# An encoder layer on one core: the last two plain steps of a Strassen block taken together by output, a lag of four, the input loaded in smaller pieces

## Chip, core and metric

The kernel runs on one core of a Trainium2 chip. The metric is the device time of one launch in microseconds (us), the median of several runs. One core has TensorE (PE in the profile), VectorE (DVE), ScalarE (ACT), GpSimd (POOL) and SyncE (SP), which here issues the loads of weights and inputs. Each engine works through its own list of instructions; across engines, semaphores make one wait for the other.

## What is computed

One layer of an encoder on 256 tokens of 2048 features in float32: a gated feed-forward part, two attention mixers side by side with a gated merge, and a second feed-forward part, each with a norm ahead of it, a norm behind it, and a residual.

```python
def rmsnorm(x, g):
    xf = x.astype(jnp.float32)
    y = xf * lax.rsqrt(jnp.mean(xf * xf, axis=-1, keepdims=True) + EPS)
    return (y * g.astype(jnp.float32)).astype(x.dtype)

def swiglu(h, w_gate, w_up, w_down):
    return (jax.nn.silu(h @ w_gate) * (h @ w_up)) @ w_down
```

The hidden width of the feed-forward parts is 5632. The change touches how the products with `w_gate` and `w_up` are run, and the first product of each of the three parts.

## The kernel before

**Products.** Every float32 number is split in two parts of lower precision, a high part (ACT casts it, L178 for weights, L359 for activations) and a low part (DVE subtracts, L180 and L361). A product is then three matmuls: high by high, low by high, high by low (L201 to L203 in ordinary blocks, L259 to L261 in wide ones). One matmul takes 128 rows of K and gives 128 tokens by 512 columns. So every unit of weights that SP loads (1 MB of float32) goes through a cast on ACT and a split on DVE before PE can use it.

**Activations.** `pre(u, h)` of `make_xT` makes, for 256 features u and token half h, what the first block of a part needs: it applies the norm and residual of the part before (L424), transposes on PE (L352), casts on ACT (L359) and splits on DVE (L361). Each second u also gives a sum of squares (L371) for the norm, which is applied later by a factor.

**Ordinary blocks.** `run_block` gives 512 columns for both token halves. Step i multiplies u = i for half 0 and u = i - lag for half 1, so that half 1 runs `lag` steps behind. `lag` is LAG (3) where a part begins with activations that must first be made (the first mixer block, the first gate block of the second feed-forward part) and where the part before ends; it is 0 in the first gate block of all.

**Wide blocks.** `run_wide` gives 1024 columns at once: four outputs of 128 tokens by 512 columns, named P2, P3 (half 0), Q4 and X (half 1). In the gate and up blocks with odd number (1, 3, 5, 7, 9, in both feed-forward parts, 20 blocks) it mixes two kinds of steps, as `SKIND = "NSNSNSNN"` says: N is a plain step (24 matmuls for 256 features, six for each output), S is one step of Strassen's method, with seven products in place of eight on sums of activations (`forms`) and of weights (DVE L189 to L191). The products of all S steps gather in banks of PSUM; after the last S step, DVE combines them (L294 to L307): the product P1 is copied by ACT (a, L294), P2 gets a added (L295), and so on. Before the change two N steps follow the last S step, one after the other (block 1 of each part has its steps in another order, FIRST, and there only one N step follows). The first matmul of such a step adds to P2, and so has to wait until L295 is done. The output of a block leaves through `after` in the last step.

**What sets the order.** The code only names operations; a scheduler with priorities (`tc.high_priority`) and a queue of work put off (`later`, `pump`) sets the order on each engine when the kernel is built. Weights are asked for two units ahead (`LA`).

**Start.** At the top level, SP loads `x` in pieces of columns 0 to 256, 256 to 1024 and 1024 to 2048 for each half, and between them four quarters of the first unit of weights.

Of the kernel before, what the change touches and what calls it, by code (L numbers as in the profile page):

```python
# [29 lines left out]
NEG = -1e30  # L30
OFF_QA, OFF_KV, OFF_QB, OFF_KB, OFF_VB, OFF_GA, OFF_GB = 0, 1024, 1536, 2560, 3584, 4608, 6656
KU = D // (2 * P)
LAG = 3
LAG_END = 3
LA = 2
SKIND = "NSNSNSNN"
FIRST = (0, 2, 1, 4, 3, 6, 5, 7)
HP = 300
AHEAD = 2
PARTS = ((0, 3), (3, 7), (7, 11))  # L40
WARM = 7
# [3 lines left out]
def encoder_layer(  # L45
# [27 lines left out]
    def acc_tile():  # L73
        return accp.tile([P, NC], F32, tag="acc", name=nm("acc"))
# [121 lines left out]
    def weights(k):  # L196
        emit_upto(k + LA)
        return emitted[k]
# [28 lines left out]
    def run_block(start, nu, lhs, after, lag=0, pre=None, tail=None):  # L227

        acc = [acc_tile(), acc_tile()]
        for i in range(nu + lag):  # L230
            if pre is not None:
                if i == 0:
                    pre(0, 0)
                    if not lag:
                        pre(0, 1)
                if i + 1 < nu:
                    pre(i + 1, 0)
                k = i - lag if lag else i + 1
                if 0 <= k < nu:
                    pre(k, 1)  # L240
            if tail is not None and i == nu + lag - 1:
                tail(0, 0)
            for h, u in ((0, i), (1, i - lag)):
                if not 0 <= u < nu:
                    continue
                whi, wlo = weights(start + u // 2)
                t = lhs(u, h)
                for j in range(2):
                    q = 2 * (u % 2) + j
                    mm3(acc[h], t[:, 0, j, :], t[:, 1, j, :], whi[:, q, :], wlo[:, q, :],  # L250
                        u == 0 and j == 0, u == nu - 1 and j == 1)
                if u == nu - 1:
                    with tc.high_priority(HP):
                        after(h, 0, acc[h])
            if i % 2:
                pump()

    def mm3s(o, t, w, q, first, last, skip=False):
        nc.tensor.matmul(o, t[0], w[0][:, q, :], start=first, stop=False, skip_group_check=skip)  # L259
        nc.tensor.matmul(o, t[1], w[0][:, q, :], start=False, stop=False, skip_group_check=skip)  # L260
        nc.tensor.matmul(o, t[0], w[1][:, q, :], start=False, stop=last, skip_group_check=skip)  # L261

    def run_wide(block, lhs, forms, after):
# [3 lines left out]
        last_s = max([n for n, (_, k) in enumerate(steps) if k == "S"], default=-1)  # L267
        bank, opened = {}, set()
        end = len(steps) - 1

        def open_(o):
            if o not in bank:
                bank[o] = acc_tile()
            f = o not in opened
            opened.add(o)
            return f

        for n, (u, kind) in enumerate(steps):
            w = weights(start + n)
            if kind == "S":  # L280
# [10 lines left out]
                if n == last_s:  # L291
                    with tc.high_priority(HP):
                        a, u2, v = t2(), t2(), t2()
                        nc.scalar.copy(a, bank["P1"])  # L294
                        nc.vector.tensor_tensor(bank["P2"], bank["P2"], a, ALU.add)  # L295
                        nc.vector.tensor_tensor(u2, bank["P6"], a, ALU.add)
                        nc.vector.tensor_tensor(v, bank["Q5"], u2, ALU.subtract)
                        nc.vector.tensor_tensor(bank["P3"], bank["P3"], v, ALU.add)
                        nc.vector.tensor_tensor(u2, bank["P7"], u2, ALU.add)
                        if "X" in bank:  # L300
                            nc.vector.tensor_tensor(v, bank["Q5"], u2, ALU.subtract)
                            nc.vector.tensor_tensor(bank["X"], bank["X"], v, ALU.add)
                        else:
                            nc.vector.tensor_tensor(bank["P1"], bank["Q5"], u2, ALU.subtract)
                            bank["X"] = bank["P1"]
                            opened.add("X")
                        nc.vector.tensor_tensor(bank["Q4"], bank["Q4"], u2, ALU.add)  # L307
            else:
                order = (("P2", 0, 0), ("P3", 0, 1), ("X", 1, 1), ("Q4", 1, 0)) if last_s >= 0 else                     (("P2", 0, 0), ("P3", 0, 1), ("Q4", 1, 0), ("X", 1, 1))
                for o, h, c in order:  # L310
                    t = lhs(u, h)
                    for j in range(2):
                        f = open_(o)
                        closes = n == end or n == last_s - 1 and o == "X"
                        mm3s(bank[o], (t[:, 0, j, :], t[:, 1, j, :]), w, 2 * j + c, f, closes and j == 1, last_s >= 0)
                    if n == end:
                        with tc.high_priority(HP):
                            after(h, c, bank[o])
            pump()

    def half_of(t, u, h):
# [258 lines left out]
    for h in range(2):  # L580
        x_sb[h] = big([D], F32)
    load_x(0, 0, 256)
    load_unit(0, (0, 1))
    load_x(1, 0, 256)
    for h in range(2):
        load_x(h, 256, 1024)
    load_unit(0, (2, 3))
    for h in range(2):
        load_x(h, 1024, 2048)
    load_upto(2)  # L590
# [343 lines left out]
```

## Time and profile before

| | us |
|---|---|
| median of 3 runs | 2073.56 (2073.42 to 2074.51) |
| the profiled execution | 2074.24 |
| its span in the trace | 2072.5 |
| PE busy | 2036.4 (98%) |
| DVE busy | 1434.4 (69%) |
| ACT busy | 986.9 (48%) |

The profiled execution is 0.7 us above the median; 1.7 us of it lie outside the span. PE is the engine that hardly rests, so the time can be lowered only where PE rests, runs at a lower clock, or works without need. Its clock is 2.4 GHz where the granted clock is 1.00, and 1.2 GHz at 0.50.

### The profile page before, as it was taken

Reading aid. Unit: us, or ns where it says so; the run is one execution under the profiler, and the core shown is the slowest. Engines: PE = TensorE matmul, PEld = TensorE weight load, DVE = VectorE, ACT = ScalarE, POOL = GpSimd, SP = SyncE. Lnnn points to the kernel's source line nnn. Section 1 sums busy time; section 2 is a strip of 40 time slices with the busy share of each in tenths; the row PEclk is TensorE's granted clock in tenths of the full one; section 3 lists DMA queues with packets and bytes.
Section 4 is the critical chain, followed back from the end, with each engine's and each line's share of the span. In section 5 each row is a group of like instructions: output and inputs, shape, how many; then the busy total and the mean of one; then the engine's idle time right before and its main releaser. Section 6 shows DMA issues by size and latency. Waiting matters only on the chain. (4 is left out here: it accounts for less than half of the span.)

```text
span 2072.5 us, 22867 instructions
## 1 busy us (share of the span) xinstructions
PE 2036.4 (98%) x9193; PEld 1676.8 (81%) x9193; DVE 1434.4 (69%) x1413; ACT 986.9 (48%) x956; POOL 55.5 (3%) x91
## 2 busy tenths in 40 slices
PE   9999999999999999999999999999999999999997
PEld 6888887888878878888888888778888888888886
DVE  6984798647986675676665555659658885588854
ACT  7544555435554453455454344446345544455442
POOL 1000000000000010000000000000000000000000
PEclk9999999999999999999999999999999999999999
DMA  8556555666558546554545556546575655756672
GB/s 293 187 200 214 196 184 202 223 206 201 182 203 304 205 168 206 191 175 163 193 153 183 193 196 245 200 150 203 184 245 180 222 205 187 220 182 216 238 252 87
DMA packets 140570, 416.36 MB, mean 201 GB/s; under 512 B 8414, under 2 KB 9232, under 8 KB 139184
## 3 DMA queue, kind: packets, MB, share of 16 engines
q1 hardware_dynamic: 133872, 391.15, 54.7%
q0 software_dynamic: 6560, 23.75, 4.3%
q8 instruction: 72, 1.18, 0.2%
q14 instruction: 34, 0.28, 0.0%
q10 hardware_dynamic: 32, 0.01, 0.0%
HBM read 400.19 MB, written 14.68 MB: 200 GB/s over the span
## 5 line engine op out<-in xcount | busy, mean ns | idle before, releaser
L180 DVE TENSOR_TENSOR w<-raw,w 128x2048 fp32r<-128x2048 f32 (+3 forms) x376 | 797.1, 2125 | 482.3 <-ACT w L178 480.5
L178 ACT CAST w<-raw 128x2048 fp32r<-128x2048 f32 (+3 forms) x376 | 667.7, 1782 | 746.0 <-PE acc L260 580.3
L259 PE MATMUL acc<-w,xT 128*128 128x512 f32 x1368 | 537.0, 393 | 6.4 <-DVE acc L295 6.3
L260 PE MATMUL acc<-w,xT 128*128 128x512 f32 x1368 | 533.6, 390 | 0.0
L261 PE MATMUL acc<-w,xT 128*128 128x512 f32 x1368 | 515.5, 390 | 0.0
L260 PE MATMUL acc<-w,big 128*128 128x512 f32 x828 | 323.5, 391 | 0.0
L259 PE MATMUL acc<-w,big 128*128 128x512 f32 x828 | 322.7, 390 | 0.0
L261 PE MATMUL acc<-w,big 128*128 128x512 f32 x828 | 317.9, 390 | 0.2 <-DVE w L180 0.2
L259 PEld LDWEIGHTS acc<-w,xT 128*128 128x128 f32 x1368 | 256.8, 188 | 63.0 <-DVE acc L295 9.0
L261 PEld LDWEIGHTS acc<-w,xT 128*128 128x128 f32 x1368 | 256.9, 188 | 53.3
L260 PEld LDWEIGHTS acc<-w,xT 128*128 128x128 f32 x1368 | 256.9, 188 | 51.3
L261 PEld LDWEIGHTS acc<-w,big 128*128 128x128 f32 x828 | 155.4, 188 | 33.0 <-DVE w L180 1.3
L259 PEld LDWEIGHTS acc<-w,big 128*128 128x128 f32 x828 | 155.4, 188 | 32.5 <-ACT w L178 0.3
L260 PEld LDWEIGHTS acc<-w,big 128*128 128x128 f32 x828 | 155.5, 188 | 31.9
L178 ACT CAST big<-raw 128x2048 fp32r<-128x2048 f32 (+1 forms) x64 | 118.8, 1860 | 98.3 <-DVE raw L191 94.2
L180 DVE TENSOR_TENSOR big<-raw,big 128x2048 fp32r<-128x2048 f32 (+1 forms) x64 | 141.3, 2221 | 23.6 <-ACT big L178 18.0
L202 PE MATMUL acc<-w,xT 128*128 128x512 f32 x208 | 82.9, 402 | 4.2 <-DVE xT L361 4.0
L201 PE MATMUL acc<-w,xT 128*128 128x512 f32 x208 | 84.3, 408 | 1.6 <-ACT xT L359 1.6
L203 PE MATMUL acc<-w,xT 128*128 128x512 f32 x208 | 80.6, 398 | 0.1
L201 PE MATMUL acc<-w,big 128*128 128x512 f32 x192 | 74.4, 389 | 0.0
L202 PE MATMUL acc<-w,big 128*128 128x512 f32 x192 | 74.4, 389 | 0.0
L189 DVE TENSOR_TENSOR raw<-raw 128x1024 f32<-128x1024 f32 x60 | 73.4, 1223 | 1.1
(186 smaller groups left out, 1736.4 us busy)
## 6 DMA issues: line engine op xcount, KB each, us to landing
raw<-in_ffn_w_down SPq DMA_DIRECT2D x88, 1024.0 KB, 5.1
raw<-in_w_in SPq DMA_DIRECT2D x68, 1024.0 KB, 5.0
raw<-in_ffn_w_up SPq DMA_DIRECT2D x58, 1024.0 KB, 5.1
raw<-in_ffn_w_gate SPq DMA_DIRECT2D x57, 1024.0 KB, 5.6
raw<-in_ffn_w_gate SPq DMA_DIRECT2D x60, 512.0 KB, 4.7
raw<-in_ffn_w_up SPq DMA_DIRECT2D x60, 512.0 KB, 4.6
raw<-in_w_out SPq DMA_DIRECT2D x16, 1024.0 KB, 5.0
f_dram<-t POOLq DMA_DIRECT2D x32, 256.0 KB, 6.0
```

Of the source, the lines that this page charges most:

```text
L178: nc.scalar.copy(hi[:, sl], raw[:, sl])
L180: nc.vector.tensor_tensor(lo[:, sl], raw[:, sl], f32(hi[:, sl]), ALU.subtract)
L189: nc.vector.tensor_tensor(raw[:, 1::2], raw[:, 1:3], raw[:, 3:4].to_broadcast([P, 2, NC]), ALU.add)
L201: nc.tensor.matmul(o, lhi, rhi, start=first, stop=False)
L202: nc.tensor.matmul(o, llo, rhi, start=False, stop=False)
L203: nc.tensor.matmul(o, lhi, rlo, start=False, stop=last)
L259: nc.tensor.matmul(o, t[0], w[0][:, q, :], start=first, stop=False, skip_group_check=skip)
L260: nc.tensor.matmul(o, t[1], w[0][:, q, :], start=False, stop=False, skip_group_check=skip)
L261: nc.tensor.matmul(o, t[0], w[1][:, q, :], start=False, stop=last, skip_group_check=skip)
```

## The change

Three things are edited.

1. **`run_wide`.** The last two N steps (`joint`, wherever the last S step is third from the end: 18 of the 20 blocks) are run as one. The X part of the first of them comes first (6 matmuls), then P2, P3 and Q4, each with both steps (12 matmuls), then X of the second. The sum into X on DVE is put behind that first X part, and X now always has a bank of its own. Each output is handed to `after` when its own 12 matmuls are done.
2. **`run_block`.** LAG is 4. The calls of `pre` are made through `ahead`, one step earlier for half 1.
3. **The first loads.** x comes in columns 0 to 256, 256 to 512, 512 to 1024 and 1024 to 2048, and the quarters of the first weights are put between them otherwise.

```diff
--- before.py
+++ after.py
@@ -30,12 +30,13 @@
 NEG = -1e30
 OFF_QA, OFF_KV, OFF_QB, OFF_KB, OFF_VB, OFF_GA, OFF_GB = 0, 1024, 1536, 2560, 3584, 4608, 6656
 KU = D // (2 * P)
-LAG = 3
+LAG = 4
 LAG_END = 3
 LA = 2
 SKIND = "NSNSNSNN"
 FIRST = (0, 2, 1, 4, 3, 6, 5, 7)
 HP = 300
+HC = {"P2": (0, 0), "P3": (0, 1), "Q4": (1, 0), "X": (1, 1)}
 AHEAD = 2
 PARTS = ((0, 3), (3, 7), (7, 11))
 WARM = 7
@@ -227,20 +228,26 @@
     def run_block(start, nu, lhs, after, lag=0, pre=None, tail=None):
 
         acc = [acc_tile(), acc_tile()]
+
+        def ahead(i):
+            if i + 1 < nu:
+                pre(i + 1, 0)
+            if 0 <= i + 1 - lag < nu:
+                pre(i + 1 - lag, 1)
+
         for i in range(nu + lag):
             if pre is not None:
                 if i == 0:
                     pre(0, 0)
-                    if not lag:
-                        pre(0, 1)
-                if i + 1 < nu:
-                    pre(i + 1, 0)
-                k = i - lag if lag else i + 1
-                if 0 <= k < nu:
-                    pre(k, 1)
+                if i == lag:
+                    pre(0, 1)
+                if i or lag:
+                    ahead(i)
             if tail is not None and i == nu + lag - 1:
                 tail(0, 0)
             for h, u in ((0, i), (1, i - lag)):
+                if pre is not None and not i and h and not lag:
+                    ahead(0)
                 if not 0 <= u < nu:
                     continue
                 whi, wlo = weights(start + u // 2)
@@ -267,6 +274,7 @@
         last_s = max([n for n, (_, k) in enumerate(steps) if k == "S"], default=-1)
         bank, opened = {}, set()
         end = len(steps) - 1
+        joint = last_s == end - 2 and last_s > 0
 
         def open_(o):
             if o not in bank:
@@ -297,25 +305,32 @@
                         nc.vector.tensor_tensor(v, bank["Q5"], u2, ALU.subtract)
                         nc.vector.tensor_tensor(bank["P3"], bank["P3"], v, ALU.add)
                         nc.vector.tensor_tensor(u2, bank["P7"], u2, ALU.add)
-                        if "X" in bank:
-                            nc.vector.tensor_tensor(v, bank["Q5"], u2, ALU.subtract)
+                        nc.vector.tensor_tensor(bank["Q4"], bank["Q4"], u2, ALU.add)
+                        nc.vector.tensor_tensor(v, bank["Q5"], u2, ALU.subtract)
+            elif n == end and joint:
+                continue
+            else:
+                both = [(u, w)] + ([(steps[end][0], weights(start + end))] if joint and n == end - 1 else [])
+                seq = [(o, both) for o in ("P2", "P3", "Q4", "X")]
+                if n == last_s + 1 and last_s >= 0:
+                    seq = [("X", both[:1]), *seq[:3], ("X", both[1:])]
+                ends = n == end or len(both) == 2
+                for i, (o, part) in enumerate(seq):
+                    h, c = HC[o]
+                    for q, (uu, ww) in enumerate(part):
+                        t = lhs(uu, h)
+                        for j in range(2):
+                            f = open_(o)
+                            stop = j == 1 and (i == 0 and o == "X" or ends and q == len(part) - 1)
+                            mm3s(bank[o], (t[:, 0, j, :], t[:, 1, j, :]), ww, 2 * j + c, f, stop, last_s >= 0)
+                    if i == 0 and o == "X":
+                        with tc.high_priority(HP):
                             nc.vector.tensor_tensor(bank["X"], bank["X"], v, ALU.add)
-                        else:
-                            nc.vector.tensor_tensor(bank["P1"], bank["Q5"], u2, ALU.subtract)
-                            bank["X"] = bank["P1"]
-                            opened.add("X")
-                        nc.vector.tensor_tensor(bank["Q4"], bank["Q4"], u2, ALU.add)
-            else:
-                order = (("P2", 0, 0), ("P3", 0, 1), ("X", 1, 1), ("Q4", 1, 0)) if last_s >= 0 else                     (("P2", 0, 0), ("P3", 0, 1), ("Q4", 1, 0), ("X", 1, 1))
-                for o, h, c in order:
-                    t = lhs(u, h)
-                    for j in range(2):
-                        f = open_(o)
-                        closes = n == end or n == last_s - 1 and o == "X"
-                        mm3s(bank[o], (t[:, 0, j, :], t[:, 1, j, :]), w, 2 * j + c, f, closes and j == 1, last_s >= 0)
-                    if n == end:
+                    elif ends:
                         with tc.high_priority(HP):
                             after(h, c, bank[o])
+                    if len(both) == 2 and o == "P2":
+                        pump()
             pump()
 
     def half_of(t, u, h):
@@ -580,11 +595,14 @@
     for h in range(2):
         x_sb[h] = big([D], F32)
     load_x(0, 0, 256)
-    load_unit(0, (0, 1))
+    load_unit(0, (0,))
     load_x(1, 0, 256)
+    load_unit(0, (1,))
     for h in range(2):
-        load_x(h, 256, 1024)
+        load_x(h, 256, 512)
     load_unit(0, (2, 3))
+    for h in range(2):
+        load_x(h, 512, 1024)
     for h in range(2):
         load_x(h, 1024, 2048)
     load_upto(2)
```

How the order moves. PE has as many matmuls as before. **PE at the end of gate block 5 of the first feed-forward part**: `acc_345` is P2 and `acc_348` X before; `acc_347` is P2, `acc_349` Q4 and `acc_350` X after; `w_371` and `w_374` are the units of the last two N steps. Before:

```order
L260 MATMUL acc_348_2215<-w_363_2279,xT_40_270 128x512
L261 MATMUL acc_348_2215<-w_364_2280,xT_40_270 128x512
L259 MATMUL acc_348_2215<-w_363_2279,xT_40_270 128x512
L260 MATMUL acc_348_2215<-w_363_2279,xT_40_270 128x512
L261 MATMUL acc_348_2215<-w_364_2280,xT_40_270 128x512
L410 MATMUL tp_382_2441<-ident_81,t2_340_2178 128x128 x4
L259 MATMUL acc_345_2194<-w_371_2344,xT_51_334 128x512
L260 MATMUL acc_345_2194<-w_371_2344,xT_51_334 128x512
L261 MATMUL acc_345_2194<-w_372_2345,xT_51_334 128x512
L259 MATMUL acc_345_2194<-w_371_2344,xT_51_334 128x512
L260 MATMUL acc_345_2194<-w_371_2344,xT_51_334 128x512
L261 MATMUL acc_345_2194<-w_372_2345,xT_51_334 128x512
```

After, X of the first N step, which is run among the last products of the S step:

```order
L425 MATMUL tp_388_2453<-ident_81,t2_340_2180 128x128 x4
L268 MATMUL acc_350_2225<-w_372_2347,xT_51_336 128x512
L266 MATMUL acc_350_2225<-w_371_2346,xT_51_336 128x512
L267 MATMUL acc_350_2225<-w_371_2346,xT_51_336 128x512
L268 MATMUL acc_350_2225<-w_372_2347,xT_51_336 128x512
```

and, some rows below, P2 with both:

```order
L267 MATMUL acc_349_2218<-w_363_2281,xT_40_272 128x512
L268 MATMUL acc_349_2218<-w_364_2282,xT_40_272 128x512
L266 MATMUL acc_347_2204<-w_371_2346,xT_51_336 128x512
L267 MATMUL acc_347_2204<-w_371_2346,xT_51_336 128x512
L268 MATMUL acc_347_2204<-w_372_2347,xT_51_336 128x512
L266 MATMUL acc_347_2204<-w_371_2346,xT_51_336 128x512
L267 MATMUL acc_347_2204<-w_371_2346,xT_51_336 128x512
L268 MATMUL acc_347_2204<-w_372_2347,xT_51_336 128x512
```

P2 is no longer the first output that the last N steps touch; it comes six matmuls later, and takes both steps in a row.

**DVE at the same place** (L295, after the change L303, adds a to P2; L180 is L181 after). Before:

```order
L190 TENSOR_TENSOR raw_365_2307<-raw_365_2307 128x512
L180 TENSOR_TENSOR w_372_2345<-raw_370_2342,w_371_2344 128x2048
L180 TENSOR_TENSOR w_375_2375<-raw_373_2372,w_374_2374 128x2048
L191 TENSOR_TENSOR raw_365_2307<-raw_365_2307 128x512
L295 TENSOR_TENSOR acc_345_2194<-acc_345_2194,t2_376_2399 128x512
L412 TENSOR_TENSOR big_351_2230<-tp_382_2441,big_351_2230 128x4x128
L180 TENSOR_TENSOR w_381_2414<-raw_379_2411,w_380_2413 128x2048
L180 TENSOR_TENSOR big_369_2318<-raw_365_2307,big_368_2317 128x2048
```

After:

```order
L181 TENSOR_TENSOR w_372_2347<-raw_370_2344,w_371_2346 128x2048
L191 TENSOR_TENSOR raw_365_2309<-raw_365_2309 128x512
L181 TENSOR_TENSOR big_357_2251<-raw_353_2240,big_356_2250 128x2048
L303 TENSOR_TENSOR acc_347_2204<-acc_347_2204,t2_376_2401 128x512
L192 TENSOR_TENSOR raw_365_2309<-raw_365_2309 128x512
L181 TENSOR_TENSOR w_375_2377<-raw_373_2374,w_374_2376 128x2048
L427 TENSOR_TENSOR big_342_2190<-tp_388_2453,big_342_2190 128x4x128
L181 TENSOR_TENSOR big_369_2320<-raw_365_2309,big_368_2319 128x2048
L181 TENSOR_TENSOR w_381_2415<-raw_379_2412,w_380_2414 128x2048
```

The sum into P2 now stands ahead of the split of `w_375` (the last N step's weights), and behind that of `big_357` (weights of the last S step's sums).

**ACT in the first 25 us.** The names ahead are `xT` for a cast of activations (L359, L374 after), `t` for a sum of squares, and `w_177` (before) or `w_164` (after) for the second unit of weights. Before:

```order
L359 ACTIVATE xT_235<-tp_232,gT 128x128 x2
L359 ACTIVATE xT_235<-tp_240,gT 128x128 x2
L178 CAST w_177<-raw_124 128x1024 x2
L359 ACTIVATE xT_270<-tp_267,gT 128x128 x2
L371 ACTIVATE t_42_294,pns_12_139<-big_111 128x512
L359 ACTIVATE xT_270<-tp_275,gT 128x128 x2
L371 ACTIVATE t_43_296,pns_18_151<-big_112 128x512
L359 ACTIVATE xT_301<-tp_298,gT 128x128 x2
L359 ACTIVATE xT_301<-tp_306,gT 128x128 x2
L359 ACTIVATE xT_334<-tp_331,gT 128x128 x2
L359 ACTIVATE xT_334<-tp_339,gT 128x128 x2
L178 CAST w_183<-raw_126 128x1024 x2
```

After:

```order
L374 ACTIVATE xT_237<-tp_234,gT 128x128 x2
L374 ACTIVATE xT_237<-tp_242,gT 128x128 x2
L374 ACTIVATE xT_272<-tp_269,gT 128x128 x2
L386 ACTIVATE t_42_296,pns_12_141<-big_111 128x512
L374 ACTIVATE xT_272<-tp_277,gT 128x128 x2
L386 ACTIVATE t_43_298,pns_18_153<-big_112 128x512
L374 ACTIVATE xT_303<-tp_300,gT 128x128 x2
L374 ACTIVATE xT_303<-tp_308,gT 128x128 x2
L374 ACTIVATE xT_336<-tp_333,gT 128x128 x2
L386 ACTIVATE t_53_360,pns_12_141<-big_111 128x512
L374 ACTIVATE xT_336<-tp_341,gT 128x128 x2
L179 CAST w_164<-raw_126 128x1024
```

Between the cast for `tp_240` (`tp_242` after) and the first cast of the second unit now stand 12 casts of activations and 3 sums of squares that stood behind it.

**DVE at the first mixer block**, where half 1 lags (L180, L361, L424, L412 are L181, L376, L439, L427 after). Before:

```order
L653 TENSOR_TENSOR t2_821_5302<-t2_821_5302,t2_822_5303 128x512
L180 TENSOR_TENSOR w_804_5194<-raw_802_5191,w_803_5193 128x2048
L361 SCALAR_TENSOR_TENSOR xT_800_5178<-tp_824_5317,gT_86,xT_800_5178 128x128 x2
L424 SCALAR_TENSOR_TENSOR big_735_4780<-big_693_4482,qr_778_5073,big_735_4780 128x256
L361 SCALAR_TENSOR_TENSOR xT_806_5213<-tp_825_5331,gT_86,xT_806_5213 128x128 x2
```

After:

```order
L671 TENSOR_TENSOR t2_821_5298<-t2_821_5298,t2_822_5299 128x512
L181 TENSOR_TENSOR w_804_5190<-raw_802_5187,w_803_5189 128x2048
L376 SCALAR_TENSOR_TENSOR xT_800_5174<-tp_824_5313,gT_86,xT_800_5174 128x128 x2
L439 SCALAR_TENSOR_TENSOR big_735_4782<-big_695_4492,qr_778_5075,big_735_4782 128x256
L376 SCALAR_TENSOR_TENSOR xT_806_5209<-tp_825_5327,gT_86,xT_806_5209 128x128 x2
```

The same operations stand in the same order, with lag 3 and with lag 4; apart from a swap here and there so it is for the rows around them, on PE and ACT too, and in the first gate block of the second feed-forward part.

## Rows read from the trace of the kernel before

**Rows 1.** The page's first part: busy time, share of span, instructions.

```profile
PE 2036.4 (98%) x9193; PEld 1676.8 (81%) x9193; DVE 1434.4 (69%) x1413; ACT 986.9 (48%) x956; POOL 55.5 (3%) x91
```

**Rows 2.** PE's waits, whole span: us in total, times, longest us.

```profile
PE acc L259 <- DVE acc L295: 6.3, 8, 1.3
PE acc L202 <- DVE xT L361: 4.3, 4, 1.8
PE acc L201 <- ACT xT L359: 3.9, 2, 2.3
...
PE tp L352 <- DVE big L424: 2.0, 1, 2.0
```

**Rows 3.** Timeline, PE, end of gate block 3 (start, duration, [idle before]).

```profile
241.56 0.39 PE L261 MATMUL acc<-big,xT 128*128 128x512 f32 x1
...
242.14 0.40 PE L260 MATMUL acc<-w,xT 128*128 128x512 f32 x1
242.85 0.50 PE L259 MATMUL acc<-w,xT 128*128 128x512 f32 x1 [0.31 <-DVE acc L295]
...
243.41 0.39 PE L261 MATMUL acc<-w,xT 128*128 128x512 f32 x1
```

**Rows 4.** Timeline, PE, end of gate block 5.

```profile
322.83 0.39 PE L261 MATMUL acc<-w,xT 128*128 128x512 f32 x1
...
323.74 0.60 PE L410 MATMUL tp<-ident,t 128*128 128x128 f32 x4
325.61 0.50 PE L259 MATMUL acc<-w,xT 128*128 128x512 f32 x1 [1.27 <-DVE acc L295]
...
331.34 0.96 PE L261 MATMUL acc<-big,big 128*128 128x512 f32 x3 [0.41 <-DVE big L180]
...
332.37 0.40 PE L259 MATMUL acc<-w,xT 128*128 128x512 f32 x1
```

**Rows 5.** Timeline, DVE, at the ends of gate blocks 3 and 5.

```profile
242.10 0.69 DVE L295 TENSOR_TENSOR acc<-acc,t 128x512 f32<-128x512 f32 x1
...
314.12 1.75 DVE L180 TENSOR_TENSOR w<-raw,w 128x1536 fp32r<-128x1536 f32 x1
...
317.06 2.29 DVE L180 TENSOR_TENSOR big<-raw,big 128x2048 fp32r<-128x2048 f32 x1
...
319.86 4.49 DVE L180 TENSOR_TENSOR w<-raw,w 128x2048 fp32r<-128x2048 f32 x2
...
324.86 0.70 DVE L295 TENSOR_TENSOR acc<-acc,t 128x512 f32<-128x512 f32 x1
```

**Rows 6.** Windows: us, busy us (instructions) of PE, PEld, DVE, ACT, POOL; clock; DMA.

```profile
325.50:332.00 6.50, 5.98 (x27) 4.65 (x28) 5.85 (x6) 4.25 (x4) 0.00 (x0) 1.00 0.84 296
...
761.10:764.60 3.50, 3.50 (x11) 2.73 (x10) 1.98 (x3) 3.04 (x5) 0.58 (x1) 0.51 0.95 316
```

**Rows 7.** Timeline, PE, the first block.

```profile
10.44 0.78 PE L201 MATMUL acc<-w,xT 128*128 128x512 f32 x1
...
13.14 0.63 PE L201 MATMUL acc<-w,xT 128*128 128x512 f32 x1
...
18.39 1.47 PE L352 MATMUL tp<-ident,big 128*128 128x128 f32 x12
19.61 0.48 PE L201 MATMUL acc<-w,xT 128*128 128x512 f32 x1
...
37.40 0.39 PE L202 MATMUL acc<-w,xT 128*128 128x512 f32 x1
```

**Rows 8.** Timeline, ACT, the first block.

```profile
15.71 0.63 ACT L371 ACTIVATE t<-big 128x512 f32<-128x512 f32 x1
...
16.32 0.62 ACT L359 ACTIVATE xT<-tp,gT 128x128 fp32r<-128x128 f32 x2
...
18.43 2.04 ACT L178 CAST w<-raw 128x1024 fp32r<-128x1024 f32 x2
```

**Rows 9.** Timeline, DVE, its first split of weights.

```profile
7.79 0.69 DVE L180 TENSOR_TENSOR w<-raw,w 128x512 fp32r<-128x512 f32 x1
```

## The prediction

> **What bounds the kernel now.** I read the page first: PE is busy 98% of the span [rows 1], so neither the loads nor DVE nor ACT set the pace over long stretches, and the question is what ends PE's few pauses. The list of its waits answers that [rows 2]. The longest entry is the wait of an N step's first matmul for L295, the sum of a into P2 behind the last S step: 8 times, 6.3 us. The other entries belong to the first blocks of the second and third part, where activations are still being made (L359, L361, L424). The timelines show what one pause of the first kind is. At the end of gate block 3 the matmul after 242.14 would follow 0.23 us later, the pace in long stretches without a wait; it starts at 242.85 [rows 3]. DVE ends L295 at 242.79 [rows 5], so the wait is real. At the end of gate block 5 PE rests 1.27 us for L295 and 0.41 us for a split of the sums of weights [rows 4].
>
> **Strassen blocks.** What the pauses cost goes by the time that the work in a stretch needs without them. From 241.56 to 243.41 PE starts five matmuls, 5 x 0.227 (that pace) = 1.14 us; the stretch takes 1.85, so 0.71 is lost [rows 3]. From 322.83 to 332.37 there are 28 matmuls of 512 columns and 8 transposes of 0.11, 7.24 us in all; the stretch takes 9.54, so 2.30 is lost [rows 4]. The eight waits [rows 2] are four of each kind: gate blocks 3 and 7 of the first feed-forward part and of the second lose 0.7, blocks 5 and 9 2.3. Together 4 x 0.71 + 4 x 2.30 = 12.0 us. The up blocks have no such wait.
>
> The change puts X of the first N step ahead of P2: six matmuls, 1.36 us. In blocks 3 and 7 nothing changes on DVE ahead of L295, so the sum is done at 242.79 and PE now asks for it at about 242.37 + 1.36 = 243.7: covered with 0.9 us to spare. In blocks 5 and 9 the order of DVE moves too. L295 stood behind two splits, 4.4 us from 319.86 on [rows 5]; now it stands behind the first of these, L191 and the split of `big_357`, 2.2 + 0.6 + 2.2 us, and the second split follows it. The first split can start where it did, or, with the split of 317.06 now behind it, up to 0.6 us sooner, 319.3 to 319.9; `big_357` is then done at 322.8 to 324.0 and the sum 0.6 later, at 323.5 to 324.6. PE used to come to P2 at 324.34 and now comes 1.3 later, less the matmuls it no longer has ahead, about 325.5: covered. `big_357` is the tighter one, since ten matmuls (2.3 us) lie between its first use and P2, so PE wants it at about 323.2. That is met at the early end, and missed by 0.8 at the late end. Of the 2.30 I therefore count 2.0 as gained (bounds 1.5 and 2.3). The 0.41 for the later split falls as well, since the split of `w_375`, which stood ahead of it, is wanted only behind P2's first half and PE is busy till then. So the gain is 4 x 0.71 + 4 x 2.0 = 10.8 us, bounds 8.8 and 12.0.
>
> What the joint step costs: the weights of the first N step are held till the last output but X, 1.36 us from the end of the block, where before they came free 5.45 us from it (24 matmuls). So the unit that takes over their place is cast 4.1 us later. By the order, 27 rows of PE (6.1 us) lie between the last use and the first use of the cast there, and 33 (7.5 us) till the split is used; the split of a unit of that size (1536) takes 1.75 us [rows 5], and its cast less than the 2.04 of a larger one [rows 8]. Some 4 us remain, and I count nothing; the rival below takes this cover away. DVE's and ACT's work is the same in amount.
>
> **Lag and calls ahead.** In these places PE waits 2.0 us for L424, and 3.9 and 4.3 for L359 and L361 [rows 2]. Right behind the longest wait for L361, 1.8 us, the clock fell: in the window 761.1 to 764.6 it was 0.51, where 3.5 us held 11 instructions, some eight matmuls' worth (3.5 / 0.43) in place of fifteen; that costs 1.6 us more. The window of 325.5 to 332.0, behind a pause of 1.27, kept 1.00 [rows 6]. The waits make 10 us, and four such windows 6.5, of both places together. A lag of four and calls one step earlier should give each activation one step more. But the order is the same as before, row by row, on DVE, ACT and PE: the scheduler had already put the calls as early as their inputs allow. The wait is for DVE, which runs the split of a unit of weights, 2.3 us, ahead of L361 in both. I count 0, bounds 0 and a few tenths either way for the swaps; that it does work is a rival.
>
> **The start.** Two things move. First, PE can begin before all of columns 256 to 1024 have landed: its first product comes when the first split of weights is done, about 8.5 [rows 9], where it was 10.44 [rows 7]. The 24 matmuls of the first unit, then paced 0.43 as at 13.14, are done by about 16.6 and were done by 18.39. Second, ACT's order: the first cast of the second unit, at 18.43 [rows 8] and the one that let PE go on at 19.61 [rows 7], now stands behind 12 more casts of activations at 0.25 us each (two in 0.62 with their tails overlapping, the next starts 0.5 later) and 3 sums of squares at 0.61 (15.71 to 16.32) [rows 8]: 3.0 + 1.8 = 4.8 us more. ACT can start its row of casts a little earlier, as PE is earlier; but its second pair waits for transposes that stand eight matmuls further down on PE. So the cast begins at about 22.6 (22.0 to 23.3) and its first half, 1.1 us, ends at 23.7; PE goes on at 23.8 instead of 19.61. The rest of the block took from 19.61 to 37.63, 18.0 us [rows 7]; four transposes of it, 0.5 us, are done ahead now. So it ends at 23.8 + 17.5 = 41.3, 3.7 us later than before. PE will have done nothing but 16 transposes between 17 and 23.8, so a window at the low clock may follow, 1.6 us as above. I take 4.2, between 3.7 and 5.3 and nearer the first, as the fall is not sure (bounds 3.1 less 0.4 for waits that go, 2.7, and 4.4 + 1.6 = 6.0); nothing later gives it back, since PE is the engine without rest.
>
> The Trainium skill bears on two points here. "TensorE: Matmul & The Clock Gate", in "What's actually happening", says that a gate set by how busy PE was recently lets through half or all of the clock: by it the low window follows, and the start costs 5.3; with the clock kept it costs 3.7. The same page, in "Architectural detail", says that ScalarE's queue is strictly first in, first out: by it the cast can't pass the activations, and the loss stands, which speaks against this part of the change.
>
> **The sum.** 2074.24 (the profiled execution) - 10.8 + 4.2 = 2067.6. That execution was 0.7 above the median, so the median comes to 2066.9. With the bounds of both terms: 2073.56 - 12.0 + 2.7 = 2064.3, and 2073.56 - 8.8 + 6.0 = 2070.8.
>
> **Rivals.** (a) The start costs nothing. If ACT's casts of activations end sooner than I think, because PE and DVE feed them sooner, only the earlier first product is left, 0 to 1.8 us of gain: 2073.56 - 10.8 - 0.9 = 2061.9. For it: PE's first product is 2 us earlier. Against it: 4.8 us of work on ACT stand in the way. (b) Lag and calls do what they say, and the pauses of both places go, or fall below the length behind which the clock dropped: 2066.9 less 16.5, 2050.4. Against it is the unchanged order. (c) The change does not do what it says in the Strassen blocks: the sum is hidden, but PE comes up against the next split (`big_357`, `w_381`) and only half the gain stays: 2073.56 - 5.4 + 4.2 = 2072.4. For it: at 331.34 such a split already ends a pause of 0.41 [rows 4]. (d) Slower: the held weights. If the casts behind them queue so long that the 4 us of cover are gone, each of the 18 joint ends gives a pause; at 0.71 each, as at the end of block 3, that is 12.8 us: 2066.9 + 12.8 = 2079.7. It decides from 0.4 us at each end on (6.6 / 18 to lose the whole gain). For it: DVE is busy to the last tenth around 320 to 325 [rows 5]. Against it: it would need a delay of over 4 us.
>
> **How the numbers follow.** Chances: my forecast 0.60, (a) 0.13, (b) 0.05, (c) 0.12, (d) 0.10. A measurement of this kernel can tell about 0.2%, 4.1 us, from no change. Faster by more than that are the forecast (but for its slow edge, 0.04), (a) and (b): 0.74. Within it are (c) and that edge: 0.16. Slower is (d): 0.10. The range takes in the forecast's bounds, (a) and (c): 2060.5 to 2072.8; (b), (d) and the ends are left out.
>
> **What would show it.** In the trace of the changed kernel, the wait for the sum into P2 (L303) should be gone from PE's list or below 1 us; the first gate block should end near 41, with ACT's first cast of the second unit at 22 to 23.5 and PE idle or on transposes ahead of it; the pauses at the first blocks of the second and third part should stand, 1.6 to 2.3 us long, each with a window at 0.5 behind it. I would be wrong if the cast comes by 20, if these pauses shrink, or if PE's list shows many new short waits in the up blocks for casts or splits of weights.

## The result, and the profile after

The changed kernel takes 2093.21 us (median of 4 runs, 2092.54 to 2096.09), the kernel before 2073.49 in the same session: a ratio of 1.0097, interval 1.0079 to 1.0114. It is 20 us slower, where 6.7 us faster had been forecast, and lies above the range.

PE's busy time hardly rose, but its waits are others. The page's first line, and PE's list of waits in the changed kernel (us in total, times, longest us):

```profile
PE 2042.2 (98%) x9193; PEld 1678.5 (80%) x9193; DVE 1433.6 (68%) x1413; ACT 987.9 (47%) x956; POOL 55.6 (3%) x91
```

```profile
PE tp L425 <- DVE t L502: 15.6, 10, 1.6
PE acc L203 <- DVE xT L376: 4.1, 4, 1.8
PE acc L202 <- ACT xT L374: 3.9, 2, 2.3
PE acc L266 <- ACT big L179: 3.3, 8, 0.4
PE acc L202 <- ACT w L179: 3.1, 1, 3.1
PE acc L266 <- DVE t L304: 2.2, 4, 0.6
```

The wait for the sum into P2 (L295, now L303), first in [rows 2], is gone. In its place stand ten waits of a transpose (L425) for L502, the output of an up block on VectorE; eight for a cast of sums on ScalarE; one of 3.1 us for a cast of weights at the start; and four for L304, the step of the combination that reads P6 last and so frees its bank of PSUM. The two entries of L376 and L374 are those of L361 and L359 in [rows 2], within 0.2 us.

What the places cost can be read from the starts of PE's matmuls: for each, the time to the next start over the usual one of its kind (0.227 us for 512 columns, 0.11 for a transpose), summed over a stretch. A row holds to some tenths; the exact choice of what is usual moves it by as much.

| us lost | before | after |
|---|---|---|
| first block | 7.7 | 14.2 |
| ends of gate blocks 3 and 7 (4) | 2.8 | 0 |
| ends of gate blocks 5 and 9 (4) | 9.3 | 3.5 |
| casts of sums in up blocks 3 to 9 (8) | 0 | 6.3 |
| transposes behind up blocks (10) | 0 | 18.1 |
| first mixer block | 9.3 | 9.4 |
| first gate block of the second feed-forward part | 11.8 | 11.6 |
| the rest | 8.3 | 6.7 |
| sum | 49.2 | 69.8 |

So 8.6 us were won at the gate blocks, as meant, and 18.1 + 6.3 + 6.5 lost. (The ten up blocks all have the early transposes: only gate block 1, not up block 1, has the other order of steps. The profiled execution, 2096.09 us, is the highest of the four; the one of before is 2074.24.)

**The transposes.** PE behind up block 3, timeline (start, duration, [idle before]):

```profile
295.33 0.84 PE L268 MATMUL acc<-big,big 128*128 128x512 f32 x3
296.01 0.39 PE L268 MATMUL acc<-big,xT 128*128 128x512 f32 x1
297.96 0.66 PE L425 MATMUL tp<-ident,t 128*128 128x128 f32 x4 [1.56 <-DVE t L502]
298.37 0.48 PE L266 MATMUL acc<-w,xT 128*128 128x512 f32 x1
298.69 0.40 PE L267 MATMUL acc<-w,xT 128*128 128x512 f32 x1
```

and VectorE there:

```profile
293.27 2.29 DVE L181 TENSOR_TENSOR w<-raw,w 128x2048 fp32r<-128x2048 f32 x1
295.76 0.69 DVE L304 TENSOR_TENSOR t<-acc,t 128x512 f32<-128x512 f32 x1 [0.20 <-PE acc L268]
296.56 0.69 DVE L305 TENSOR_TENSOR t<-acc,t 128x512 f32<-128x512 f32 x1
297.17 0.74 DVE L502 SCALAR_TENSOR_TENSOR t<-acc,pnr,t 128x512 f32<-128x512 f32 x1
```

The transposes of P2's output are set on PE ahead of twelve matmuls of the next gate block (the first at 298.37), and P3 of this block comes behind those. The weights for the twelve were split from 293.27 on, done at 295.56, and the bank for the first six came free with L304, at 296.45. But on VectorE the output stands behind that split and two steps of the combination, and ends at 297.91. From 296.01 to 298.69 2.68 us pass; two matmuls and four transposes take 0.89 of them; 1.8 are lost, ten times.

**The casts of sums.** ScalarE in up block 3, and PE:

```profile
281.73 1.92 ACT L179 CAST w<-raw 128x2048 fp32r<-128x2048 f32 x1 [5.44 <-PE acc L267]
283.56 1.90 ACT L179 CAST big<-raw 128x2048 fp32r<-128x2048 f32 x1
```

```profile
284.71 0.39 PE L267 MATMUL acc<-w,xT 128*128 128x512 f32 x1
285.51 0.50 PE L266 MATMUL acc<-big,big 128*128 128x512 f32 x1 [0.41 <-ACT big L179]
```

The cast of the first N step's weights stands ahead of the cast of the sums, and waits 5.44 us for PE to free a buffer. In the kernel before it stood behind:

```profile
274.25 1.92 ACT L178 CAST big<-raw 128x2048 fp32r<-128x2048 f32 x1 [0.68 <-DVE raw L191]
276.07 1.91 ACT L178 CAST w<-raw 128x2048 fp32r<-128x2048 f32 x1
```

**The start.** ScalarE, PE, and the window behind (us, busy us of PE, PEld, DVE, ACT, POOL, clock, DMA):

```profile
22.79 0.73 ACT L374 ACTIVATE xT<-tp,gT 128x128 fp32r<-128x128 f32 x2
23.29 1.16 ACT L179 CAST w<-raw 128x1024 fp32r<-128x1024 f32 x1
```

```profile
20.93 0.44 PE L367 MATMUL tp<-ident,big 128*128 128x128 f32 x2 [0.69 <-DVE xT L376]
24.50 0.79 PE L202 MATMUL acc<-w,xT 128*128 128x512 f32 x1 [3.13 <-ACT w L179]
```

```profile
24.40:30.40 6.00, 5.90 (x14) 4.64 (x15) 5.09 (x12) 6.00 (x15) 2.12 (x5) 0.50 0.32 85
```

The cast that let PE go on at 19.61 [rows 7] now starts at 23.29 in place of 18.43 [rows 8], PE goes on at 24.50, and for these 6 us its clock is at the lower of its two levels.

### The profile page after: what moved, and what is told of

The parts are those of the page before. It is cut to its first block, busy times and chain, and to the rows that moved or that the text cites. A ratio compares the mean times of both kernels' runs of the same rounds, so it can differ in the third digit from the quotient of the medians.

```text
span 2094.3 us, 22890 instructions
## 1 busy us (share of the span) xinstructions
PE 2042.2 (98%) x9193; PEld 1678.5 (80%) x9193; DVE 1433.6 (68%) x1413; ACT 987.9 (47%) x956; POOL 55.6 (3%) x91
## 5 line engine op out<-in xcount | busy, mean ns | idle before, releaser
L181 DVE TENSOR_TENSOR w<-raw,w 128x2048 fp32r<-128x2048 f32 (+3 forms) x376 | 797.0, 2124 | 470.7 <-ACT w L179 414.3
L181 DVE TENSOR_TENSOR big<-raw,big 128x2048 fp32r<-128x2048 f32 (+1 forms) x64 | 141.7, 2217 | 21.1 <-ACT big L179 15.8
L266 PE MATMUL acc<-big,big 128*128 128x512 f32 x180 | 70.9, 394 | 3.3 <-ACT big L179 3.3
```

What stands on the lines that cost most here:

```text
L181: nc.vector.tensor_tensor(lo[:, sl], raw[:, sl], f32(hi[:, sl]), ALU.subtract)
```

## Experiments

Each run stands against the kernel before on the same chip; its medians there were 2074.61, 2073.83 and 2074.01 us for e1 to e4, e5 to e8 and e9 to e12.

**e1: the joint step alone.** Only `run_wide` is taken from the changed kernel; `run_block`, the lag and the loads are those of the kernel before. The first lines of the edit, against the changed kernel:

```diff
-LAG = 4
+LAG = 3
...
```

> The kernel before with the joint step alone (lag 3, old calls, old loads). Theory A: the changed kernel lost in three places that add up: 18.1 us in ten waits of transposes for L502 behind up blocks, 6.3 us in eight waits for a cast of sums of weights in up blocks, 6.5 us at the start, against 8.5 us won at the ends of gate blocks. Then this one, without the start, comes to 2073.5 - 8.5 + 18.1 + 6.3 = 2089.4 us, its PE waits ten times for L502. Theory B: the early transposes come only with the lag or the other calls; then it comes to 2073.5 + 6.3 - 8.5 = 2071.3.

2089.46 us, ratio 1.0070 (1.0055 to 1.0085). Theory A holds: 14.9 us are lost against the kernel before on this chip, where 15.9 were expected (that the time agrees to the tenth is chance, as this chip's kernel before is 1.1 us slower). Its list has the ten waits for the output (L496 here) at its head and, further down, the eight for casts.

```profile
PE tp L419 <- DVE t L496: 15.6, 10, 1.6
...
PE acc L260 <- ACT big L179: 3.3, 8, 0.4
...
PE acc L260 <- DVE t L298: 2.0, 4, 0.5
```

So neither lag nor calls nor loads have a part in these waits.

**e2: the pump.** `later(tr, 2)` puts the transposes of an output off by two calls of `pump`. In the kernel before, P2's output was handed over in the last step, and the two calls were the end of that step and the end of the next block's first. In the joint step a pump follows P2 at once and another ends the step, so P2's transposes are named one step earlier, ahead of the next block's first step. e2 moves the pump ahead of the first output.

```diff
                 ends = n == end or len(both) == 2
+                if len(both) == 2:
+                    pump()
                 for i, (o, part) in enumerate(seq):
...
-                    if len(both) == 2 and o == "P2":
-                        pump()
```

> The joint step alone, with the extra pump moved from behind P2 to ahead of the step's first output, so that the transposes put off by P2's output come out one step later, as in the kernel before. Theory A (the pump puts the transposes too early): the ten waits go, 2089.4 - 18.1 = 2071.3 us. Theory C (VectorE is late with the output because of the joint step itself, wherever the transposes stand): the wait turns up at another instruction and the time stays above 2083.

2078.39 us, ratio 1.0019 (1.0010 to 1.0029): 11 us less than e1. The ten waits are gone, none has come behind the up blocks: Theory A, not C. But it isn't the 18 us expected, and the list tells where the rest is:

```profile
PE acc L260 <- DVE t L298: 6.4, 4, 1.6
PE tp L361 <- DMA big<-in_x: 5.9, 3, 4.2
PE acc L260 <- ACT big L179: 5.9, 12, 0.7
```

The scheduler set gate blocks 5 and 9 anew. VectorE there, and the first matmul of the next block:

```profile
321.53 0.69 DVE L297 TENSOR_TENSOR acc<-acc,t 128x512 f32<-128x512 f32 x1
322.13 2.28 DVE L181 TENSOR_TENSOR w<-raw,w 128x2048 fp32r<-128x2048 f32 x1
...
331.92 2.29 DVE L181 TENSOR_TENSOR w<-raw,w 128x2048 fp32r<-128x2048 f32 x1 [1.91 <-ACT w L179]
334.13 0.68 DVE L298 TENSOR_TENSOR t<-acc,t 128x512 f32<-128x512 f32 x1
```

```profile
334.96 0.47 PE L260 MATMUL acc<-w,xT 128*128 128x512 f32 x1 [1.60 <-DVE t L298]
```

L298 is L304 of the changed kernel, the step that frees P6's bank of PSUM; it stands behind a split that itself waits 1.91 us for its cast. These ends lose 2.95 us each here, 0.84 in e1: 4 x 2.1 = 8.4 us given back.

**e3: X first, not joined.** As e1, with one line changed.

```diff
-        joint = last_s == end - 2 and last_s > 0
+        joint = False
```

> The X part first in the first N step, but the two N steps not joined (joint = False). Theory A2 (the eight waits for casts of sums come from X being first, which pulls the cast of the N step's weights ahead of the cast of sums on ScalarE): as e2 within 2 us, about 2071, the eight waits of 0.4 us are there. Theory D (they come from weights held by the joint step): they are gone, about 2065.

2078.13 us, ratio 1.0018 (1.0009 to 1.0027), as e2. The waits are the same to the tenth:

```profile
PE acc L260 <- DVE t L298: 6.4, 4, 1.6
PE acc L260 <- ACT big L179: 5.9, 12, 0.7
```

So the weights held by the joint step are not what the casts of sums wait for. They come with the X part being first. As ScalarE's order shows, the first N step's weights are then wanted early, and the scheduler puts their cast ahead; no run put that cast back with X first, so this last link is read, not tested. Theory A2, not D.

**e4: the calls of `pre` alone.** Only `run_block` is taken, with lag 3.

> The kernel before with the calls of pre through ahead alone (lag 3, old loads, old wide blocks). Theory A: in its order the cast of the second unit of weights stands behind the casts of activations, as in the changed kernel, so the start loses its 6.5 us: 2080 us. Theory E: the loads in small pieces do it, and this one stays at 2073.5.

2076.32 us, ratio 1.0008 (0.9999 to 1.0018), between both forecasts, and as a time not clear of no change; the trace shows why. Its list has the start's wait, longer than in the changed kernel:

```profile
PE acc L202 <- ACT w L179: 4.2, 1, 4.2
...
PE acc L202 <- ACT xT L366: 2.3, 1, 2.3
```

Its first block loses 14.5 us where the kernel before loses 7.7, as theory A said. What had not been expected is a gain: one of the two waits for L359 [rows 2] is missing, and the first mixer block and the first gate block of the second feed-forward part lose 6.9 and 7.3 us, where they lost 9.3 and 11.8.

**e5: the loads alone.**

> The kernel before with the loads in small pieces alone. In its order too the first cast of the second unit of weights stands behind the casts of activations. Theory A (where that cast stands sets the start): about 6 us lost in the first block, 2080 us, though x lands earlier. Theory E (the loads alone are harmless or a gain, the calls do it): 2072 to 2074.

2079.76 us, ratio 1.0032 (1.0020 to 1.0043). Theory A: each of the two edits, the calls (e4) and the loads, alone brings the cast behind the activations. PE:

```profile
20.60 0.44 PE L353 MATMUL tp<-ident,big 128*128 128x128 f32 x2 [0.69 <-DVE xT L362]
24.17 0.80 PE L202 MATMUL acc<-w,xT 128*128 128x512 f32 x1 [3.13 <-ACT w L179]
```

**e6: the loads, with the cast held in its old place.**

```diff
-                nc.scalar.copy(hi[:, sl], raw[:, sl])
+                cast = nc.scalar.copy(hi[:, sl], raw[:, sl])
+                first_cast[k] = cast
...
-                    hi_of[h] = nc.scalar.activation(t[:, 0, j, :], tp[:, j, :], AF.Copy, scale=gs[j])
+                    with queued(first_cast.get(1) if gi == 0 and u > 3 else None):
+                        hi_of[h] = nc.scalar.activation(t[:, 0, j, :], tp[:, j, :], AF.Copy, scale=gs[j])
```

> As e5, but the casts of activations for u = 4 and above in the first block are held behind the cast of the second unit of weights, as they stood before. Theory A: the 6 us come back, and the earlier first product may give 1 to 2 more: 2071 to 2074. If something else in the loads costs the time, it stays near e5.

2073.88 us, ratio 0.9999 (0.9990 to 1.0008): the 6 us are back. ScalarE and PE:

```profile
19.02 2.04 ACT L180 CAST w<-raw 128x1024 fp32r<-128x1024 f32 x2
```

```profile
20.17 0.50 PE L204 MATMUL acc<-w,xT 128*128 128x512 f32 x1
```

The loads in small pieces are worth nothing here: PE's first product comes at 9.57 in place of 10.44, but it goes on at 20.17 where it did at 19.61 [rows 7].

**e7: the earlier calls only where a block lags.** The first gate block keeps the old calls, the lag stays 3.

> The calls of pre one step earlier only in the blocks that lag (lag stays 3); the first gate block has the old calls. In e4 the first blocks of the second and third part lost 6.9 and 7.3 us where they lose 9.3 and 11.8 in the kernel before. Theory F (earlier calls shorten those waits, and only the first gate block pays for them): 2073.5 - 6.7 = 2066.8 us. Theory G (these gains of e4 came from where its later start put the low-clock stretches): within 2 us of the kernel before.

2070.32 us, ratio 0.9984 (0.9975 to 0.9994): 3.5 us faster, half of what theory F said. The window behind the last wait of the first gate block of the second feed-forward part:

```profile
1357.80:1361.00 3.20, 2.76 (x13) 2.27 (x14) 1.65 (x6) 2.97 (x6) 0.58 (x1) 1.00 0.57 159
```

PE at these waits, in the kernel before and in e7:

```profile
1358.28 0.51 PE L201 MATMUL acc<-w,xT 128*128 128x512 f32 x1 [1.62 <-ACT xT L359]
1360.60 0.50 PE L202 MATMUL acc<-w,xT 128*128 128x512 f32 x1 [1.81 <-DVE xT L361]
```

```profile
1358.24 0.50 PE L202 MATMUL acc<-w,xT 128*128 128x512 f32 x1 [0.91 <-DVE xT L371]
```

There the waits of 1.62 and 1.81 us shrank to one of 0.91, no stretch at the low clock follows, and 7.6 us are lost in place of 11.8. The first mixer block loses 9.6, as before: there e4's gain was of the clock only, as theory G said.

**e8: X first in the gate blocks alone, with two holds.** The split of the last N step's weights is held behind the sum into P2 in gate blocks, and the cast of the first N step's weights behind the cast of the last sums in up blocks. For the first hold the gate blocks also ask for the last N step's weights later: at the last S step they ask one unit ahead, not two. The holds in the edit:

```diff
+                with queued(sum_cast.get(k - 1) if k in behind else None):
+                    sum_cast[k] = nc.scalar.copy(hi[:, sl], raw[:, sl])
+                with queued(p2_of.get(k) or (lo_of.get(0) if k in paced else None)):
                     nc.vector.tensor_tensor(lo[:, sl], raw[:, sl], f32(hi[:, sl]), ALU.subtract)
...
+                        p2_of[start + end] = nc.vector.tensor_tensor(bank["P2"], bank["P2"], a, ALU.add)
```

> X first in the first N step of the gate blocks alone, the two N steps not joined; in these blocks the split of the last N step's weights on VectorE is held behind the sum into P2, and in up blocks the cast of the first N step's weights on ScalarE behind the cast of the last sums. Theory H (the idea of covering the sum with X is sound, and all losses in the wide blocks come from where the casts, splits and transposes landed): the waits for the sum and the eight waits for casts go, 2073.5 - 12 = 2061.5 us. Theory I (the cover only hands the wait on): at least one of the ends of gate blocks 5 and 9 keeps over 1.5 us, and the time is above 2067.

2075.54 us, ratio 1.0010 (1.0000 to 1.0020). Neither forecast: all waits at the ends of gate blocks are gone, 5 and 9 too, but the hold in the up blocks was too strong, as e9 shows. The split of the first N step's weights now comes late there, ten times:

```profile
PE acc L264 <- DVE w L183: 9.5, 10, 1.1
```

**e9: the same with a looser hold.** The cast is held behind the sums of the last S step but one.

```diff
-                with queued(sum_cast.get(k - 1) if k in behind else None):
+                with queued(sum_cast.get(k - 3) if k in behind else None):
```

> As e8, but in up blocks the cast of the first N step's weights is held only behind the sums of the last S step but one, so that the split of these weights stands about as early as in the kernel before. e8's 9.5 us of waits for that split (ten times) should go. Theory H: the waits at the ends of gate blocks stay away as in e8, 2073.7 - 12 = 2062 us. Theory I: another cast or split of the up blocks turns up in its place, ten times 0.8 or more, and the time stays above 2068.

2068.12 us, ratio 0.9978 (0.9969 to 0.9988): 5.9 us faster than before. VectorE and PE at the end of gate block 3, to be read beside [rows 3, 5]:

```profile
239.47 0.70 DVE L358 TENSOR_TENSOR acc<-acc,t 128x512 f32<-128x512 f32 x1
```

```profile
242.41 0.39 PE L264 MATMUL acc<-big,xT 128*128 128x512 f32 x1
242.64 0.39 PE L262 MATMUL acc<-w,xT 128*128 128x512 f32 x1
```

The sum into P2 (L358) ends 2.5 us ahead of the matmul that needs it. What is missing from the 12 us are, for the most part, eight shorter waits for a split:

```profile
PE acc L264 <- DVE w L183: 4.2, 8, 0.9
```

So theory H is right on the gate blocks and theory I has its share in the up blocks.

**e10: e9 with the calls of e7.**

> e9 with the earlier calls of e7. If the two gains are of different stretches, they add up: e9 less 3.5 us, about 2058.5 us. If e9's shift in time moves the low-clock stretches, e7's gain may be smaller: within 1 us of e9.

2065.73 us, ratio 0.9961 (0.9946 to 0.9976): 2.4 us less than e9, the fastest of all, 8.3 us below the kernel before. So the two gains add up but for 1.1 us (2058.5 had been expected from e9 at 2062). The waits of the first gate block of the second part fell as in e7 (7.6 us lost there).

**e11: e9, joined by output in the gate blocks.** ScalarE's and VectorE's orders are the same as in e9.

> e9 with the two last N steps of the gate blocks joined by output; by their order ScalarE and VectorE do the same in the same order as in e9, only PE's matmuls stand otherwise. Theory J (joining costs nothing by itself, since no transposes of an output follow a gate block): within 2 us of e9. Theory D (held weights): later casts for the block behind, four or more new waits, 3 us or more above e9.

2068.97 us, ratio 0.9976 (0.9966 to 0.9985): 0.9 us above e9, and the two intervals overlap. In the gate blocks joining by output costs nothing by itself, and brings nothing. Theory J.

**e12: lag 4 alone.**

> The kernel before with a lag of four alone, old calls. With lag 4 and the earlier calls the changed kernel makes half 1 of u = i - 3 in step i, exactly as the kernel before does with lag 3 and the old calls, and its waits at the first blocks of the second and third part are the same; e7 with lag 3 and the earlier calls makes u = i - 2 and is faster. Theory K (what counts is how early these calls come): with lag 4 and old calls they come one step later, u = i - 4, but so do their matmuls; 2073.7 within 2 us. Rival: a longer lag by itself shortens the waits, 2070 or less.

2072.85 us, ratio 0.9995 (0.9986 to 1.0005): no difference in time, as theory K says. But the trace isn't that of the kernel before: in the first gate block of the second feed-forward part PE waits 3.0 us for ScalarE's casts and 2.1 for VectorE's splits of activations, where it waited 3.9 and 2.5; the wait of 1.62 us is all but gone, and only one stretch there has the low clock, where two had it. In the first mixer block a wait of 0.5 comes in. So the rival, that a longer lag by itself shortens waits, isn't refuted; what it is worth is too little for these times to tell.

## Why the prediction was wrong, point by point

**The Strassen blocks: the step "I count nothing" failed.** The gain was sized nearly rightly: 8.6 us against 10.8 forecast, just under the lower bound of 8.8. (Blocks 5 and 9 still lose 0.9 us each, behind L304 and not behind the split of `big_357` that I had feared.) The cost was not. I followed the order through the ends of two gate blocks, wrote that the up blocks have no wait, and counted nothing for the joint step, of which I looked only at the weights that it holds. In an up block the joint step does two more things, which I did not cost: it calls `pump` once more behind P2, and hands P2's output over ahead of the rest. A moved pump moves all that is put off by it, here four transposes on PE. That is the 18.1 us (e1 has the ten waits, e2 none; 8.4 of the 18.1 came back elsewhere in e2). The order of PE, read in an up block, would have shown transposes of P2's output between P2 and P3; I read it in gate blocks, where the outputs have no transposes. One of my own signs of being wrong, many new short waits in the up blocks for casts or splits, did come: the eight for casts. The ten long ones I had not foreseen at all.

**The casts of sums, 6.3 us, were a rival with the wrong mechanism.** Rival (d) had weights held by the joint step; e3 shows the same waits without the joint step, and e11 shows, in the gate blocks, the joint step without more waits. X first is what moved the casts.

**What was put right in one place came out in another.** e2 won 18.1 us and lost 8.4 at a new place (L298); e8 won the 12 of the gate blocks and lost more than 9.5 (the splits in up blocks). The scheduler settles casts, splits and combination anew, and VectorE, though busy only 69% over the whole, has little room at the ends of these blocks: in the kernel before it is busy 8.89 of the 9.54 us from 322.83 to 332.37. My rival (c) named such a wait for a split behind the sum, with a price of 5.4; in e2 it was 8.4.

**The lag: right, with a reason that I had missed.** I read from the order that nothing moves, and 9.4 and 11.6 us against 9.3 and 11.8 confirm it. The reason is plain arithmetic, as far as the calls go: with a lag of four the calls one step earlier make u = i + 1 - 4 in step i, with a lag of three the old ones make u = i - 3. The two edits cancel. e7, which has only the calls, and only in the blocks that lag, gains 3.5 us.

**The start: the mechanism right, its size low.** The cast starts at 23.29 (forecast 22.6), PE goes on at 24.50 (23.8), and the clock does fall: it is 0.95 on average from 17.50 to 24.40, where PE is busy for 2.54 of 6.90 us, and 0.50 from 24.40 to 30.40. The Trainium skill, "TensorE: Matmul & The Clock Gate" ("What's actually happening"), says that a gate lets through half of the clock when PE has lately been little busy; the trace agrees, with these two stretches. But the clock stays at 0.50 for 6 us, not for 3.5 as in [rows 6]: 14 matmuls start in it where some 26 would at 0.227 us each, a loss of 2.8 us by estimate, and I had counted a third of 1.6. 6.5 us were lost, 4.2 forecast, above the upper bound of 6.0. The lead was overrated as well: the first unit's 24 matmuls are done at 17.25, not 16.6. e5 and e6 show that it is the place of that cast: with the same loads and the cast held the 6 us are gone. The cast came only when the last of the activations ahead of it was done. The same page of the Trainium skill ("Architectural detail") says that ScalarE's queue is strictly first in, first out; the trace agrees: the cast starts at 23.29, behind the activations of 22.79, and in e6, with the same loads, at 19.02.

**The sum.** 2074.24 - 10.8 + 4.2 had two terms; four were needed: - 8.6 + 6.5 + 6.3 + 18.1 = + 22.3, against 21.9 between the two profiled executions.

## What to carry to other kernels

When a step is joined or moved, list what its bookkeeping does too: every call that releases work put off (here `pump`) moves that work, and on PE, busy 98% here, transposes that waited 1.6 us cost 1.8 us each time. Where a scheduler sets the order, read the new order at every kind of place that the edit touches, not only where the gain is meant to be. Two edits can cancel: write down the indices of both together before costing either.

## What the runs showed of the hardware that was not expected

The same pause does not always bring the low clock. Behind the waits at 1332.72 us (2.26 us in the kernel before) a stretch at 0.50 followed, while in e1, e2 and e9 the same 2.26 us had none behind it, and their first gate block of the second part lost 10.0 to 10.1 us in place of 11.8. The pauses of 1.56 us behind up blocks brought none. Two windows of the kernel before, one behind each of its two long pauses there, and one of e9, behind the same 2.26 us:

```profile
1334.60:1338.00 3.40, 3.40 (x11) 2.62 (x10) 2.22 (x7) 1.24 (x4) 0.58 (x1) 0.50 0.22 90
...
1361.90:1365.40 3.50, 3.50 (x11) 2.72 (x10) 1.64 (x1) 2.96 (x5) 0.17 (x1) 0.51 0.92 339
```

```profile
1329.20:1333.00 3.80, 3.47 (x15) 2.57 (x16) 3.52 (x11) 1.81 (x7) 0.92 (x2) 1.00 0.04 15
```

Each stretch at 0.50 is worth some 1.6 us, and the kernel before itself has now more and now fewer of them: in its last 25 runs, from 2071.63 to 2077.39 us, the mean granted clock lay between 0.993 and 0.996, and the seven runs at 0.996 have a median of 2072.47, the five at 0.993 one of 2074.73. So these stretches explain a part of the spread. The gain of e9 isn't such luck: its mean clock over ten runs, 0.9943, is no higher than that of the kernel before, 0.9946. What decides whether the clock falls stays open.
